# One decoder layer on one core: block inversion moved from VectorE to GpSimd, low parts all on VectorE, gates in one 32-column operand, a second wide group, matmul widths alternating

## The chip, the core and the metric

The kernel runs on one core of a Trainium2 chip. Its time is in microseconds (us) of the device: one execution of the whole program on that core. Three runs of the kernel before took 1485.14, 1487.25 and 1487.25 us, median 1487.25. In this document PE is TensorE, which multiplies matrices; DVE is VectorE; ACT is ScalarE; POOL is GpSimd; SP is the engine that issues most of the DMAs. A lower-case c in the rows is one of 67 general buffers.

## The reference

One decoder layer for 256 tokens of width 2048, all in float32. What matters here:

```python
proj = h @ w_in[l]                      # q, k, v, z, b, a, p
o_gdn = gated_deltanet(qkv, z, b, a, ...)   # 8 heads x 128, in chunks of 64
o_pool = multiscale_pool(p, pool_w[l], pool_scale[l])
mix = jnp.concatenate([o_gdn, o_pool], axis=-1) @ w_out[l]
h = layer_norm(DEEPNORM_ALPHA * h + mix, ...)
xa = memory_cross_attention(h, mem, xq_w[l], xk_w[l], xv_w[l], xo_w[l])
h = layer_norm(DEEPNORM_ALPHA * h + xa, ...)
ff = jnp.square(jax.nn.relu(h @ w_up[l])) @ w_down[l]
h = layer_norm(DEEPNORM_ALPHA * h + ff, ...)
...
# inside gated_deltanet, for each head and chunk:
L = jnp.where(strict, jnp.einsum("nbhcd,nbhmd->nbhcm", k_beta, k) * decay, 0.0)
sol = lax.linalg.triangular_solve(eye + L, rhs, left_side=True, lower=True, unit_diagonal=True)
```

The triangular solve is done with explicit inverses. The smallest ones are of 64 blocks of 32 x 32, one block to a partition; they are built by 31 steps of a multiplication and a subtraction, and that is the "block inversion".

## The kernel before

**Two parts of each operand.** Every float32 operand of a large matmul is split into a high part H, which ACT rounds to the fast matmul type (line 188), and a low part L = x - H, which DVE subtracts (line 189). A product is the sum H·H + H·L + L·H. One weight tile is 128 x 1024 numbers (512 KB), so one tile costs ACT one activation and DVE one subtraction. H and L tiles have 3 buffers each, the raw tile W has 4: ACT can start the split of a tile when PE has finished with the tile three places before it, so that PE has at most three tiles in hand when ACT or DVE stops. Ten of the subtractions (`POOL_W`, plan places 40 to 109, every sixth) go to POOL.

**Wide groups.** A projection group (`proj_a`) gives 512 output columns in four PSUM accumulators, from 8 weight tiles. In the wide form the activations' two parts lie side by side, so that one 512-column matmul does H·H and H·L (line 325) and one 256-column matmul does L·H (line 329). Over a tile PE does all 8 wide ones, then all 8 narrow ones; in a group's last tile it does 2 and 2 for each accumulator. The two halves of a wide accumulator are added afterwards: for most groups ACT copies it out and POOL adds (`fold`, line 203). In the narrow form, which the first two groups have, there are three 256-column matmuls (line 346).

**Groups in order.** The ten groups of `w_in` come first: two of k, two of q, two of v, two of z, two of p. Between the first two stand the gates (`gates_plan`): 48 matmuls with a 128-column weight operand in which only 16 columns are not zero. Then follow the memory's k, `w_out`, the memory's v, the queries `w_q`, `w_o`, and the MLP's up and down projections.

**What sets the order.** The work that is not a projection (convolutions, heads, inversion, solve, normalisation) is a list of generators, the background. After each weight tile `bg.step` runs them until a budget for DVE and ACT is used up (2.35 and 3.4 us a tile), counted by the costs that the generators yield, not by the clock. The order on every engine's queue is fixed when the program is built; each engine works its queue strictly in that order and waits where an operand is missing.

**The inversion.** `base_inverse` (line 709) sends the blocks through memory: eight small DMAs write `ld`, SP loads it as `lb` (line 716), DVE does the 31 steps (lines 726 and 728; step j works on (31-j)(j+1) elements, 5,456 over all steps, twice), SP stores `xd` (line 731), and ACT issues 16 small DMAs that load the result (line 735). Each of these three queues goes on only when the step before it is done. The activation of z (`silu`, line 899) is put two tiles behind the fold that it needs.

Of the kernel before, what the change touches and what calls it, by code (L numbers as in the profile page):

```python
# [15 lines left out]
P = 128  # L16
T = 256
# [30 lines left out]
POOL_W = 40, 110, 6  # L48
# [75 lines left out]
def hybrid_layer(ctx: ExitStack, tc: tile.TileContext, xT, xtok, memT, w_ba, w_in, small, w_pool,  # L124
# [59 lines left out]
    def split(h, l, src, n=0, eng=V):  # L184

        if n:
            bg.charge(.09 + 1.05e-3 * n if eng is V else 0, .1 + .84e-3 * n)
        S.activation(out=h, in_=src, func=AF.Copy)  # L188
        eng.tensor_tensor(out=l, in0=src, in1=h.bitcast(F32), op=ALU.subtract)  # L189
# [34 lines left out]
    def run():  # L224
# [24 lines left out]
        def do_split():  # L249
            i = pos["split"]  # L250
            kind, src, shape, fn = plan[i][:4]
            if kind in "fwh":
                h = wp.tile([P] + shape, F32R, tag="H", name=nm("H"), bufs=HB)
                l = wp.tile([P] + shape, F32R, tag="L", name=nm("L"), bufs=HB)
                split(h, l, raw.pop(i), shape[0] * shape[1] if len(shape) == 2 else 1024,
                      nc.gpsimd if POOL_W[0] <= i < POOL_W[1] and i % POOL_W[2] == 0 else V)
# [55 lines left out]
    def proj_a(src, acts, evac, kt_outer=False, load=None, fine=0, pre=None, wide=False, spread=False):  # L312
        accs = []

        def tile_fn(k0, ns):
            def fn(h, l):
# [6 lines left out]
                def first(s, n):  # L323
                    c = slice(n * P, (n + 1) * P)
                    mm(out=accs[n], lhsT=h[:, s, c], rhs=acts[k0 + s].wide, start=k0 + s == 0, stop=False)  # L325

                def second(s, n):
                    c = slice(n * P, (n + 1) * P)
                    mm(out=accs[n][:, :T], lhsT=l[:, s, c], rhs=acts[k0 + s][0], start=False, stop=k0 + s == KT - 1)  # L329

                if wide:

                    for part in ([[(s, n) for s in range(ns)] for n in range(4)] if last else [order]):
                        for s, n in part:
                            first(s, n)
                        for s, n in part:
                            second(s, n)
# [103 lines left out]
    nc.gpsimd.memset(m64[0:64, 64:128], 1.0)  # L441
    eps_ln = const.tile([P, 1], F32, name="eps_ln")
# [149 lines left out]
    def gates_plan():  # L592
        pb = []

        def fn(j):
            def f(h, l):
                if j == 0:
                    pb.append(acc())
                o = pb[0][:, :T]
                for s in range(8):  # L600
                    kt = 8 * j + s
                    a = xs[kt]
                    mm(out=o, lhsT=h[:, s, :], rhs=a[0], start=kt == 0, stop=False)
                    mm(out=o, lhsT=h[:, s, :], rhs=a[1], start=False, stop=False)
# [902 lines left out]
```

## Time and profile before

| | us |
|---|---|
| median of three runs | 1487.25 |
| the profiled execution | 1487.29 |
| its span | 1485.6 |
| PE busy | 1468.0 |
| DVE busy | 944.8 |
| ACT busy | 726.0 |
| POOL busy | 149.5 |

The span is the time from the first to the last instruction that the profiler saw; 1.7 us of the execution lie outside it. In a timeline a row gives the start, the duration from the first start to the last end, and a count; matmuls overlap, so the distance of two starts, not the duration of one, is what a matmul costs. The value in brackets is the idle time of the engine before the row, and what ended it.

### The profile page before, as it was taken

What the parts mean: (1) busy time and instruction counts of PE and PEld (TensorE: products, weight loads), DVE (VectorE), ACT (ScalarE), POOL (GpSimd) and SP (SyncE); (2) the same over time, 40 slices, a digit from 0 to 9 for tenths busy, and PEclk for the clock granted to TensorE, in tenths of its full rate; (3) what the DMA queues carried; (4) which work ended last, traced back from release to release, by engine and by line L of the source; (5) the groups of instructions that cost most, each with busy time, mean ns of one, the idle gap of its engine ahead of it and who ended that gap; (6) DMA issues with size and microseconds to landing.
All of it is one profiled execution on the core that took longest, in us unless ns stands there. A gap on an engine that the chain in (4) does not pass through costs nothing.

```text
span 1485.6 us, 21126 instructions
## 1 busy us (share of the span) xinstructions
PE 1468.0 (99%) x8038; PEld 1274.6 (86%) x8038; DVE 944.8 (64%) x1471; ACT 726.0 (49%) x1061; POOL 149.5 (10%) x191
## 2 busy tenths in 40 slices
PE   9999999999999999999999999999999999999996
PEld 8988889899888888998888888888888888888886
DVE  6778976867656755555685555566555565556656
ACT  6765555755533545453545444455334444345441
POOL 1024323700300000000130000000000000000001
PEclk9999999999999999999999999999999999999998
DMA  7556555535855555444735655555556655555571
GB/s 273 188 196 184 171 187 173 188 132 170 289 194 194 179 189 189 147 138 156 279 131 176 199 191 189 196 188 181 197 197 204 228 193 191 192 197 185 185 247 65
DMA packets 86758, 280.45 MB, mean 189 GB/s; under 512 B 13904, under 2 KB 14944, under 8 KB 86656
## 3 DMA queue, kind: packets, MB, share of 16 engines
q1 hardware_dynamic: 78928, 268.73, 54.1%
q0 software_dynamic: 2960, 9.58, 2.0%
q10 hardware_dynamic: 4768, 0.79, 0.3%
q8 instruction: 63, 1.03, 0.3%
q14 instruction: 39, 0.32, 0.1%
HBM read 276.43 MB, written 2.63 MB: 188 GB/s over the span
## 4 chain that ended last, share of the span: by engine, by line
PE 97%; DVE 1%; DMA 1%; ACT 1%; issue 0%; POOL 0%; ACTq 0%; POOLq 0%; DVEq 0%
PE acc L325 29%; PE acc L329 15%; PE acc L371 13%; PE acc L373 13%; PE acc L372 13%; PE acc L346 5%; PE acc L408 0%; PE acc L407 0%; PE acc L406 0%; DMA W<-w_in 0%; PE acc L1346 0%; PE acc L1344 0%; PE acc L1345 0%; PE aux L1191 0%; PE aux L1227 0%
## 5 line engine op out<-in xcount | busy, mean ns | idle before, releaser
L189 DVE TENSOR_TENSOR L<-W,H 128x1024 fp32r<-128x1024 f32 x469 | 579.0, 1236 | 465.4 <-ACT H L188 461.7
L188 ACT ACTIVATE H<-W 128x1024 fp32r<-128x1024 f32 x479 | 507.4, 1059 | 587.4 <-PE acc L373 301.5
L325 PE MATMUL acc<-c,H 128*128 128x512 f32 x1920 | 499.5, 394 | 1.1 <-DVE c L189 0.6
L325 PEld LDWEIGHTS acc<-c,H 128*128 128x128 f32 x1920 | 338.3, 189 | 56.8 <-ACT c L200 1.7
L371 PE MATMUL acc<-H,c 128*128 128x512 f32 x832 | 325.3, 391 | 0.0
L373 PE MATMUL acc<-H,c 128*128 128x512 f32 x832 | 323.9, 389 | 0.0
L372 PE MATMUL acc<-L,c 128*128 128x512 f32 x832 | 323.9, 389 | 0.0
L329 PEld LDWEIGHTS acc<-c,L 128*128 128x128 f32 x1920 | 274.2, 190 | 27.2
L329 PE MATMUL acc<-c,L 128*128 128x256 f32 x1920 | 281.4, 282 | 0.0
L373 PEld LDWEIGHTS acc<-H,c 128*128 128x128 f32 x832 | 156.2, 188 | 32.8
L372 PEld LDWEIGHTS acc<-L,c 128*128 128x128 f32 x832 | 156.3, 188 | 31.7
L371 PEld LDWEIGHTS acc<-H,c 128*128 128x128 f32 x832 | 156.2, 188 | 31.8
L203 POOL TENSOR_TENSOR c<-c 128x256 f32<-128x256 f32 x60 | 48.8, 839 | 372.5 <-ACT c L200 372.5
L189 DVE TENSOR_TENSOR c<-c,c 128x256 fp32r<-128x256 f32 (+1 forms) x170 | 76.6, 503 | 10.3 <-ACT c L188 10.3
L188 ACT ACTIVATE c<-c 128x256 fp32r<-128x256 f32 (+1 forms) x170 | 66.5, 455 | 2.5 <-DMA c<-xT 2.5
L346 PE MATMUL acc<-c,H 128*128 128x256 f32 x384 | 66.3, 288 | 1.1 <-ACT H L188 1.1
L1062 POOL DMA_DIRECT2D c<-lnrow x24 | 12.9, 540 | 518.4 <-PE acc L373 345.7
L346 PEld LDWEIGHTS acc<-c,H 128*128 128x128 f32 x384 | 57.8, 196 | 2.1 <-ACT H L188 1.8
L346 PE MATMUL acc<-c,L 128*128 128x256 f32 x192 | 47.6, 287 | 0.0
L200 ACT ACTIVATE c<-acc 128x512 f32<-128x512 f32 x60 | 35.6, 599 | 18.9 <-PE acc L329 15.0
L531 DVE SCALAR_TENSOR_TENSOR c<-c,par 128x255 f32<-128x255 f32 (+2 forms) x72 | 38.1, 538 | 3.6 <-ACT c L528 1.9
L217 ACT ACTIVATE c<-acc 128x256 f32<-128x256 f32 x60 | 23.0, 384 | 23.0 <-PE acc L329 23.0
(241 smaller groups left out, 1005.5 us busy)
## 6 DMA issues: line engine op xcount, KB each, us to landing
W<-w_up SPq DMA_DIRECT2D x127, 512.0 KB, 3.5
W<-w_down SPq DMA_DIRECT2D x120, 512.0 KB, 3.4
W<-w_in SPq DMA_DIRECT2D x76, 512.0 KB, 3.4
W<-w_k SPq DMA_DIRECT2D x32, 512.0 KB, 3.3
W<-w_out SPq DMA_DIRECT2D x32, 512.0 KB, 4.2
W<-w_v SPq DMA_DIRECT2D x32, 512.0 KB, 3.2
W<-w_q SPq DMA_DIRECT2D x32, 512.0 KB, 3.3
W<-w_o SPq DMA_DIRECT2D x24, 512.0 KB, 3.3
```

The source lines that it names most:

```text
L188: S.activation(out=h, in_=src, func=AF.Copy)
L189: eng.tensor_tensor(out=l, in0=src, in1=h.bitcast(F32), op=ALU.subtract)
L200: S.activation(out=ab.rearrange("p s c -> p (s c)"), in_=o, func=AF.Copy)
L203: nc.gpsimd.tensor_tensor(out=r, in0=ab[:, 0, :], in1=ab[:, 1, :], op=ALU.add)
L217: S.activation(out=r, in_=o[:, :T], func=AF.Copy)
L325: mm(out=accs[n], lhsT=h[:, s, c], rhs=acts[k0 + s].wide, start=k0 + s == 0, stop=False)
L329: mm(out=accs[n][:, :T], lhsT=l[:, s, c], rhs=acts[k0 + s][0], start=False, stop=k0 + s == KT - 1)
L346: mm(out=accs[n][:, :T], lhsT=w[:, s, n * P:(n + 1) * P], rhs=acts[kt][x], start=kt == 0 and w is h and x == 0, stop=kt == KT - 1 and w is l)
L371: mm(out=accs[t], lhsT=a[0][:, c], rhs=h, start=kt == 0, stop=False)
L372: mm(out=accs[t], lhsT=a[0][:, c], rhs=l, start=False, stop=False)
L373: mm(out=accs[t], lhsT=a[1][:, c], rhs=h, start=False, stop=kt == KT - 1)
L531: V.scalar_tensor_tensor(out=u[:, sh:], in0=x[:, :T - sh], scalar=w[:, 3 - sh:4 - sh], in1=u[:, sh:], op0=ALU.mult, op1=ALU.add)
```

## The change

Five edits. The 31 steps of the inversion are issued on POOL in place of DVE, and the generator gives the turn back after every 1.8 us of its own counting. All low parts are subtracted by DVE. The gates' operand shrinks to 16 columns, whose high and low parts stand side by side in one 32-column operand: 16 matmuls of 512 columns, then 4 small ones with a matrix of two identities (`twos`) that add up the parts and transpose. The second group of `w_in` becomes wide. From the queries on, a group's tiles take turns (`turn`): a tile that follows one which ended with narrow matmuls starts with narrow ones, but for the first tile of a group.

```diff
-    def split(h, l, src, n=0, eng=V):
+    def split(h, l, src, n=0):
         if n:
-            bg.charge(.09 + 1.05e-3 * n if eng is V else 0, .1 + .84e-3 * n)
+            bg.charge(.09 + 1.05e-3 * n, .1 + .84e-3 * n)
         S.activation(out=h, in_=src, func=AF.Copy)
-        eng.tensor_tensor(out=l, in0=src, in1=h.bitcast(F32), op=ALU.subtract)
+        V.tensor_tensor(out=l, in0=src, in1=h.bitcast(F32), op=ALU.subtract)
...
             kind, src, shape, fn = plan[i][:4]
-            if kind in "fwh":
+            if kind in "wh" and shape == [KT, 16]:
+                h = wp.tile([P, KT, 32], F32R, tag="H", name=nm("H"), bufs=HB)
+                split(h[:, :, 0:16], h[:, :, 16:32], raw.pop(i), KT * 16)
+                parts[i] = (h, None)
+            elif kind in "fwh":
                 h = wp.tile([P] + shape, F32R, tag="H", name=nm("H"), bufs=HB)
                 l = wp.tile([P] + shape, F32R, tag="L", name=nm("L"), bufs=HB)
-                split(h, l, raw.pop(i), shape[0] * shape[1] if len(shape) == 2 else 1024,
-                      nc.gpsimd if POOL_W[0] <= i < POOL_W[1] and i % POOL_W[2] == 0 else V)
+                split(h, l, raw.pop(i), shape[0] * shape[1] if len(shape) == 2 else 1024)
                 parts[i] = (h, l)
...
-                def first(s, n):
+                def first(s, n, ends):
                     c = slice(n * P, (n + 1) * P)
-                    mm(out=accs[n], lhsT=h[:, s, c], rhs=acts[k0 + s].wide, start=k0 + s == 0, stop=False)
-                def second(s, n):
+                    mm(out=accs[n], lhsT=h[:, s, c], rhs=acts[k0 + s].wide, start=k0 + s == 0,
+                       stop=ends and k0 + s == KT - 1)
+                def second(s, n, ends):
                     c = slice(n * P, (n + 1) * P)
-                    mm(out=accs[n][:, :T], lhsT=l[:, s, c], rhs=acts[k0 + s][0], start=False, stop=k0 + s == KT - 1)
+                    mm(out=accs[n][:, :T], lhsT=l[:, s, c], rhs=acts[k0 + s][0], start=False,
+                       stop=ends and k0 + s == KT - 1)
...
                     for part in ([[(s, n) for s in range(ns)] for n in range(4)] if last else [order]):
-                        for s, n in part:
-                            first(s, n)
-                        for s, n in part:
-                            second(s, n)
+                        low = turn and width[0] == "low" and k0 > 0
+                        for step in (second, first) if low else (first, second):
+                            for s, n in part:
+                                step(s, n, step is (first if low else second))
+                        width[0] = "high" if low else "low"
                         if last:
...
     nc.gpsimd.memset(m64[0:64, 64:128], 1.0)
+    twos = const.tile([P, 16], F32, name="twos")
+    V.tensor_tensor(out=twos, in0=ident[:, 0:16], in1=ident[:, 16:32], op=ALU.add)
     eps_ln = const.tile([P, 1], F32, name="eps_ln")
...
     def gates_plan():
-        pb = []
-        def fn(j):
-            def f(h, l):
-                if j == 0:
-                    pb.append(acc())
-                o = pb[0][:, :T]
-                for s in range(8):
-                    kt = 8 * j + s
-                    a = xs[kt]
-                    mm(out=o, lhsT=h[:, s, :], rhs=a[0], start=kt == 0, stop=False)
-                    mm(out=o, lhsT=h[:, s, :], rhs=a[1], start=False, stop=False)
-                    mm(out=o, lhsT=l[:, s, :], rhs=a[0], start=False, stop=kt == KT - 1)
-                if j == 1:
-                    ba.append(chunk([T]))
-                    S.activation(out=ba[0], in_=o, func=AF.Copy)
-                    bg.event("ba")
-            return f
-        for j in range(2):
-            add("w", w_ba[j], [8, P], fn(j))
+        def fn(hl, _):
+            o = acc()
+            for kt in range(KT):
+                mm(out=o[0:32, :], lhsT=hl[:, kt, :], rhs=xs[kt].wide, start=kt == 0, stop=kt == KT - 1)
+            ba.append(chunk([2, T]))
+            S.activation(out=ba[0][0:32].rearrange("p s c -> p (s c)"), in_=o[0:32, :], func=AF.Copy)
+            bg.event("ba")
+        add("w", w_ba, [KT, 16], fn)
...
         for a in range(NT):
-            nc.tensor.transpose(out=pt[:, a * P:(a + 1) * P], in_=ba[0][:, a * P:(a + 1) * P], identity=ident)
+            for s in range(2):
+                mm(out=pt[:, a * 16:a * 16 + 16], lhsT=ba[0][0:32, s, a * P:(a + 1) * P], rhs=twos[0:32, :],
+                   start=s == 0, stop=s == 1)
         yield 0, .2, 1
-        ptv = pt[:, :T].rearrange("p (a c) -> p a c", a=NT)
+        ptv = pt[:, :2 * 16].rearrange("p (a c) -> p a c", a=NT)
         e = small_tile(sh)
...
         u = small_tile(sh)
-        V.tensor_tensor(out=u, in0=ptv[:, :, 32:40],
+        V.tensor_tensor(out=u, in0=ptv[:, :, 8:16],
                         in1=par[:, C_DT:C_DT + 8].unsqueeze(1).to_broadcast([P, NT, HEADS]), op=ALU.add)
...
         yield 0, 0, 2
+        load = 0
         for j in range(31):
...
             t = tb[:, :n * (j + 1)].rearrange("p (n c) -> p n c", n=n)
-            V.tensor_tensor(out=t, in0=lb[:, j, j + 1:32].unsqueeze(2).to_broadcast([NB, n, j + 1]),
-                            in1=xb[:, j, 0:j + 1].unsqueeze(1).to_broadcast([NB, n, j + 1]), op=ALU.mult)
-            V.tensor_tensor(out=xb[:, j + 1:32, 0:j + 1], in0=xb[:, j + 1:32, 0:j + 1], in1=t,
-                            op=ALU.subtract)
-            yield .3 + 2.1e-3 * n * (j + 1), 0, 0
+            nc.gpsimd.tensor_tensor(out=t, in0=lb[:, j, j + 1:32].unsqueeze(2).to_broadcast([NB, n, j + 1]),
+                                    in1=xb[:, j, 0:j + 1].unsqueeze(1).to_broadcast([NB, n, j + 1]), op=ALU.mult)
+            nc.gpsimd.tensor_tensor(out=xb[:, j + 1:32, 0:j + 1], in0=xb[:, j + 1:32, 0:j + 1], in1=t,
+                                    op=ALU.subtract)
+            load += .3 + 4.6e-3 * n * (j + 1)
+            if load > 1.8:
+                load = 0
+                yield 0, 0, 1
         nc.sync.dma_start(out=xd, in_=xb)
...
         bg.add(f"k{h}", k_head(h), f"x{h}")
-    proj_a(w_in[1], xs, conv_evac(4))
+    proj_a(w_in[1], xs, conv_evac(4, True), wide=True)
     bg.add("base", base_inverse(), *[f"k{h}" for h in range(HEADS)])
...
                 bg.event(f"Q{4 * g + n}")
-        proj_a(w_q[g], f1, q_evac, wide=g < 3, kt_outer=g == 0, pre={0: ["ln1_0", "ln1_1"]} if g == 0 else None)
+        proj_a(w_q[g], f1, q_evac, wide=g < 3, turn=True, kt_outer=g == 0, pre={0: ["ln1_0", "ln1_1"]} if g == 0 else None)
         bg.add(f"att{g}", attend(g), *[f"Q{4 * g + n}" for n in range(4)])
...
                     bg.urgent.append(finish(g, rs, hid))
-            proj_a(w_up[4 * qd + g], f2, u_evac, wide=True, spread=True)
+            proj_a(w_up[4 * qd + g], f2, u_evac, wide=True, spread=True, turn=True)
         for g in range(4):
...
     b, a, p = wi[:, 4096:4104], wi[:, 4104:4112], wi[:, 4112:]
-    wba = np.zeros((D, P), wi.dtype)
-    wba[:, 0:8] = b
-    wba[:, 32:40] = a
+    wba = np.concatenate([b, a], axis=1)
     cw = f(conv_w)[0].reshape(4, 3, 8, P)[:, [1, 0, 2]]
```

Line numbers in the rows of the changed kernel are its own: 188 is the subtraction there, 187 the high part, 202 the fold, 541 a convolution's step, 904 the silu of z, 728 and 730 the inversion, 740 the loads of its result.

DVE's queue, inside the inversion. L_ with a number is the low part of one weight tile; tb, lb and xb belong to the inversion; before:

```order
L189 TENSOR_TENSOR L_2031<-W_1914,H_2030 128x1024
L726 TENSOR_TENSOR tb<-lb,xb 64x255
L728 TENSOR_TENSOR xb<-xb,tb 64x15x17
L726 TENSOR_TENSOR tb<-lb,xb 64x252
L728 TENSOR_TENSOR xb<-xb,tb 64x14x18
L726 TENSOR_TENSOR tb<-lb,xb 64x247
```

Now, at the same place (541 is a convolution, 590 to 595 a query head):

```order
L188 TENSOR_TENSOR L_1940<-W_1784,H_1939 128x1024
L541 SCALAR_TENSOR_TENSOR c_1320<-c_1320,par 128x255
L541 SCALAR_TENSOR_TENSOR c_1320<-c_1320,par 128x254
L541 SCALAR_TENSOR_TENSOR c_1320<-c_1320,par 128x253
L188 TENSOR_TENSOR L_1977<-W_1813,H_1976 128x1024
L590 COPY ssq<-aux_1966 128x2
L593 SCALAR_TENSOR_TENSOR c_1059<-aux_1965,cc,c_1059 128x256
L595 SCALAR_TENSOR_TENSOR c_1059<-aux_1965,cc,c_1059 128x128
```

Between two low parts there stood up to ten instructions of the inversion; now there stand convolutions and query heads, which used to come after it.

POOL's queue, around the fold of the first z group (c_2142 and c_2157 there, c_2175 and c_2190 now); before:

```order
L203 TENSOR_TENSOR c_1944<-c_1945 128x256
L189 TENSOR_TENSOR L_2055<-W_1956,H_2054 128x1024
L203 TENSOR_TENSOR c_2142<-c_2143 128x256
L203 TENSOR_TENSOR c_2142<-c_2150 128x256
L203 TENSOR_TENSOR c_2157<-c_2158 128x256
L203 TENSOR_TENSOR c_2157<-c_2165 128x256
L189 TENSOR_TENSOR L_2233<-W_2112,H_2232 128x1024
```

Now:

```order
L728 TENSOR_TENSOR tb<-lb,xb 64x156
L730 TENSOR_TENSOR xb<-xb,tb 64x6x26
L202 TENSOR_TENSOR c_2175<-c_2176 128x256
L202 TENSOR_TENSOR c_2175<-c_2183 128x256
L202 TENSOR_TENSOR c_2190<-c_2191 128x256
L202 TENSOR_TENSOR c_2190<-c_2198 128x256
L728 TENSOR_TENSOR tb<-lb,xb 64x135
L730 TENSOR_TENSOR xb<-xb,tb 64x5x27
L728 TENSOR_TENSOR tb<-lb,xb 64x112
```

The four folds of z stood behind a low part; now 26 of the 31 steps of the inversion stand ahead of them, and five behind.

ACT's queue, from the silu of that z group to the loads of the inverse; before:

```order
L188 ACTIVATE H_2202<-W_2086 128x1024
L899 ACTIVATE c_2142<-c_2142 128x256 x2
L899 ACTIVATE c_2157<-c_2157 128x256 x2
L188 ACTIVATE H_2232<-W_2112 128x1024
L534 ACTIVATE c_614<-c_1143 128x256
L528 ACTIVATE c_1389<-c_1389,par 128x256
L528 ACTIVATE c_1397<-c_1397,par 128x256
L188 ACTIVATE H_2274<-W_2136 128x1024
L188 ACTIVATE H_2299<-W_2176 128x1024
L735 DMA c_1748<-xd 32x4x32
```

Now:

```order
L187 ACTIVATE H_2256<-W_2088 128x1024
L904 ACTIVATE c_2175<-c_2175 128x256 x2
L904 ACTIVATE c_2190<-c_2190 128x256 x2
L797 ACTIVATE c_2008<-aux_2240,sv 128x128
L797 ACTIVATE c_2009<-aux_2240,sv 128x128
L544 ACTIVATE c_2246<-c_1857 128x256
L544 ACTIVATE c_2251<-c_1865 128x256
L187 ACTIVATE H_2289<-W_2129 128x1024
L740 DMA c_1645<-xd 32x4x32
L740 DMA c_1649<-xd 32x4x32
L740 DMA c_1645<-xd 32x4x32
L740 DMA c_1649<-xd 32x4x32
```

In both the silu stands two tiles behind the evacuation. The loads from xd stood behind three more high parts; now they stand behind one, H_2289, which itself stands behind the silu.

## Rows read from the trace of the kernel before

**Rows 1.** The page: busy us by engine (share of the span), instructions.
```profile
PE 1468.0 (99%) x8038; PEld 1274.6 (86%) x8038; DVE 944.8 (64%) x1471; ACT 726.0 (49%) x1061; POOL 149.5 (10%) x191
```

**Rows 2.** Timeline of PE in an up projection: start us, us, what, count.
```profile
1002.09 2.00 PE L325 MATMUL acc<-c,H 128*128 128x512 f32 x8
1003.93 1.11 PE L329 MATMUL acc<-c,L 128*128 128x256 f32 x8
1004.88 2.00 PE L325 MATMUL acc<-c,H 128*128 128x512 f32 x8
...
1007.68 0.63 PE L325 MATMUL acc<-c,H 128*128 128x512 f32 x2
1008.37 0.63 PE L325 MATMUL acc<-c,H 128*128 128x512 f32 x2
```

**Rows 3.** Timeline of PE, 512-column matmuls alone, 54 starts apart.
```profile
699.63 0.39 PE L371 MATMUL acc<-H,c 128*128 128x512 f32 x1
...
711.87 0.39 PE L371 MATMUL acc<-H,c 128*128 128x512 f32 x1
```

**Rows 4.** Timeline of PE: three narrow matmuls from one start to the other.
```profile
36.02 0.40 PE L346 MATMUL acc<-c,H 128*128 128x256 f32 x2
...
36.38 0.40 PE L346 MATMUL acc<-c,H 128*128 128x256 f32 x2
```

**Rows 5.** One window, 145:191.7: line 726 alone, line 728 alone, all engines.
```profile
145.00:191.70 46.70, 19.95 (x31) 1.00 0.52 169
...
145.00:191.70 46.70, 12.11 (x31) 1.00 0.52 169
...
145.00:191.70 46.70, 46.70 (x273) 41.18 (x272) 45.01 (x76) 24.42 (x32) 18.70 (x13) 1.00 0.52 169
```

**Rows 6.** Timeline of POOL: adds of 1024 and of 256 elements.
```profile
116.36 2.40 POOL L189 TENSOR_TENSOR L<-W,H 128x1024 fp32r<-128x1024 f32 x1 [6.34 <-ACT H L188]
...
288.77 2.81 POOL L203 TENSOR_TENSOR c<-c 128x256 f32<-128x256 f32 x4
```

**Rows 7.** Timeline of DVE and POOL where both work at once.
```profile
269.71 2.33 DVE L531 SCALAR_TENSOR_TENSOR c<-c,par 128x255 f32<-128x255 f32 x3
271.84 1.43 POOL L942 TENSOR_TENSOR c<-c 128x256 f32<-128x256 f32 x2
...
282.40 4.44 DVE L189 TENSOR_TENSOR L<-W,H 128x1024 fp32r<-128x1024 f32 x3
284.22 1.54 POOL L942 TENSOR_TENSOR c<-c 128x256 f32<-128x256 f32 x1
```

**Rows 8.** Timeline of DVE and of SP's queue: the inversion's start, its result's store.
```profile
145.13 1.27 DVE L726 TENSOR_TENSOR tb<-lb,xb 64x31 f32<-64x31 f32 x1
...
191.62 0.46 SPq L731 DMA_DIRECT2D xd<-xb  x1
```

**Rows 9.** Timeline of ACT around the first z group, then its loads of the inverse.
```profile
177.73 2.69 ACT L200 ACTIVATE c<-acc 128x512 f32<-128x512 f32 x4 [0.54 <-PE acc L329]
180.32 1.06 ACT L188 ACTIVATE H<-W 128x1024 fp32r<-128x1024 f32 x1
...
182.63 1.32 ACT L899 ACTIVATE c<-c 128x256 f32<-128x256 f32 x4
...
195.01 1.76 ACTq L735 DMA_DIRECT2D c<-xd  x4
```

**Rows 10.** Timeline of PE: one query head's matmuls, then two waits.
```profile
139.43 0.59 PE L575 MATMUL aux<-c 128*128 128x256 f32 x2
...
140.44 1.86 PE L325 MATMUL acc<-c,H 128*128 128x512 f32 x7
...
202.44 0.61 PE L578 MATMUL aux<-ones,c 128*128 128x1 f32 x4 [0.23 <-ACT c L571]
...
206.41 0.98 PE L325 MATMUL acc<-c,H 128*128 128x512 f32 x3 [0.47 <-ACT c L200]
```

**Rows 11.** Timeline of PE at the start, clock not yet granted in full.
```profile
5.58 2.07 PE L346 MATMUL acc<-c,H 128*128 128x256 f32 x8 [1.13 <-ACT H L188]
```

More of the change, by code (lines that the diff above doesn't have):

```diff
@@ L47 @@
 HOLD, KEEP = 3, 1
-POOL_W = 40, 110, 6
 RLA, XLA, RD = 7, 14, 6
@@ L309, in add, with proj_a @@
         plan.append((kind, src, shape, fn, pre, post))
-    def proj_a(src, acts, evac, kt_outer=False, load=None, fine=0, pre=None, wide=False, spread=False):
+    width = ["low"]
+    def proj_a(src, acts, evac, kt_outer=False, load=None, fine=0, pre=None, wide=False, spread=False, turn=False):
         accs = []
@@ L1481, in _layout @@
         "xT": feat(x), "xtok": f(x)[0].reshape(NT, P, D), "memT": feat(mem),
-        "w_ba": wba.reshape(2, 8, P, P).transpose(0, 2, 1, 3),
+        "w_ba": wba.reshape(KT, P, 16).transpose(1, 0, 2),
         "w_in": tiles(np.concatenate([k, q, v, z, p], axis=1)), "small": small, "w_pool": pw,
```

## The prediction, made before the change was run

> **What bounds the kernel now.** I read the page's busy shares first: PE works 1468.0 of 1485.6 us, 99%, every other engine 64% or less [rows 1]. So the end comes earlier only through fewer or cheaper matmuls, or a wait of PE that goes; and anything that leaves PE without a weight tile comes out on the clock in full. Next, what a matmul costs, from distances of starts: 54 of 512 columns in 711.87 − 699.63 = 12.24 us, 226.7 ns each [rows 3]; three of 256 columns in .36 us, 120 ns each [rows 4]. A full wide tile takes 1.84 us for its 8 wide and .95 for its 8 narrow ones, 2.79 together [rows 2]. Then the one stretch where other engines are full: from 145 to 191.7 DVE works 45.0 of 46.7 us, and the inversion's two lines are 19.95 + 12.11 = 32.1 us of it [rows 5]. Last ACT, SP and PE just behind that stretch: the store of the inverse at 191.62, its loads at 195.01, and two short waits of PE [rows 8 to 10].
>
> **The change part by part.** The sum is made against the profiled execution, 1487.29 us (span 1485.6 and 1.7 outside); the median of the runs, 1487.25, is the same number for this purpose.
>
> *Gates.* 48 × .120 = 5.76 us become 16 × .227 = 3.63, −2.1. Four small matmuls take the place of two transposes; four one-column matmuls take .61 us [rows 10]. The new ones are bounded by 0 and about .8; I take +.4, so −1.7 (−2.1 to −1.3).
>
> *Second group wide.* 64 times three narrow matmuls, .360, become one wide and one narrow, 2.79/8 = .349: −.7 us (0 to −.9). Its four evacuations get folds on POOL, counted below.
>
> *Alternating widths.* In a full tile 2.79 us stands against 8 × .2267 + 8 × .120 = 2.774, so a change from narrow to wide and back costs .016 us (the first step alone, 1.84 − 1.814, .026). In a group's last tile two and two take 1008.37 − 1007.68 = .69, the plain sum [rows 2], so nothing goes there. About three changes between full tiles go in each of 18 groups (three of the queries, fifteen up): 54 × .016 = −.9 us, bounds 0 and −1.4. L is now wanted before H every second tile; it lies ready one tile ahead, and where PE never waits for it that costs nothing.
>
> *Two waits of PE,* .23 and .47 us [rows 10], both behind ACT work that follows the inverse: −.7 if ACT comes earlier, 0 if not.
>
> *DVE* loses 32.1 us and gets the ten low parts back, and conv steps and query heads that stood behind the inversion move into its place. That is about as much as it can do there before PE needs it; I cost it at nothing, since the low parts are first in each tile's share and a tile's is 1.5 us of 2.79 even beside a busy POOL (4.44 for three) [rows 7]. Without that cover it would be late by up to the 4 us by which the moved work could exceed the stretch.
>
> These are −1.7 − .7 − .9 − .7 = −4.0: without any new stall 1483.3.
>
> *The inversion on POOL* is the part that decides. POOL's price: 2.40 us for 1024 elements and 2.81/4 = .70 for 256 [rows 6], so 2.2 ns an element and .13 to .17 us an instruction (two in a chain take 1.43 [rows 7]). The first op came at 145.13 [rows 8]; less the gates' gain 143.5. In POOL's queue steps 0 to 25, 5,031 elements twice, stand ahead of the z folds: 10,062 × 2.2 ns = 22.1, and 52 × .17 = 8.9; with four folds of v and four of z at .70, 5.6 together, 36.6 us if POOL is alone. It is not alone. A 256-element add beside a low part takes 1.54 in place of .70, so one low part costs POOL .84 [rows 7]. Fourteen low parts stand in that stretch of DVE's queue: 12 us. A conv step costs POOL little (two adds that begin under the last of three take 1.43, against 1.40): 27 of them 2 us. So the last fold of z ends at F = 143.5 + 36.6 + 14 = 194.1, bounds 180.1 (no contention at all) and 199 (each low part blocks for its whole time, next paragraph).
>
> The Trainium skill, "SBUF — State Buffer", section "SBUF: two separate sides", says that VectorE with two SBUF inputs and GpSimd hold their common port as an exclusive lock for a whole instruction. The rows show a loss of .84 for one low part, where the low part alone would be (4.44 − .70)/3 = 1.25. By that rule 14 × 1.25 = 17.5 in place of 12, F = 199.6.
>
> Who waits for F: ACT. The silu of z waits for the folds, and behind it stand four copies and the high part H_2289. Evacuation of that group was at 177.73 [rows 9]; it moves by −2.4 (gates, second group), by six query heads that now come before it, 140.44 − 139.43 = 1.0 each [rows 10], and .4 of value heads: 181.7. ACT got to the silu 4.9 us after that [rows 9], so 186.6. PE then has three tiles in hand, 8.4 us: it needs H_2289 at 195.0. ACT gives it F + .66 (half of the four silus' 1.32) + 1.5 (four copies, as the silus) + 1.06 [rows 9] = F + 3.2 = 197.3: **PE stands 2.4 us** (none if F is below 191.8). Next: five steps of the inversion on POOL, 3.7 us with their waits, then the store; store to loads 195.01 − 191.62 = 3.4 [rows 8, 9]; four loads' issue 1.76 [rows 9]; two copies .8 and the next high part 1.06: H_2317 at F + 11.0 with some .3 between them. PE has tile H_2289 done at F + 6.2: **4.8 us more**. The following tiles have four loads each ahead of their high part, 1.76 + .8 + 1.06 = 3.6 against PE's 2.79: **.8 more** before the loads are through. Before the change the same loads came after three more high parts, and PE lived on these.
>
> Sum: 1487.29 − 4.0 + 2.4 + 4.8 + .8 = **1491.3, slower**. Its own range, with F by ±3 us (contention .65 to 1.05 a low part, start ±1): 1488 to 1496.
>
> **The rivals.**
> (a) *Hidden.* POOL is done in time, F below 186.8 (then H_2317 at F + 11.0 comes before PE has finished the tile of H_2289, at 195.0 + 2.8 = 197.8): 1483.3, with the small gains at their ends 1481.5 to 1485.5. For it: two lone collisions are all that the rows show of contention, and ACT's lead over PE is reckoned, not read; against it: a low part would have to cost POOL no more than (186.8 − 182.1)/14 = .33, not .84.
> (b) *Half.* F from 187 to 191.5: no wait at the silu, up to 4.7 us at the loads: 1483.5 to 1488.8, about no change; at 189.5 it is 2.7 + .8, 1486.8.
> (c) *Port and clock, on the other side far out.* F is 199.6 and the long stalls cost PE more than themselves: 2.4 + 5.5 = 7.9, 4.8 and .8 us. At the start, before PE's clock is granted in full, eight 256-column matmuls take over .2 us each where .12 is the steady price [rows 11]; 16 such after each of two stalls are 2.8 us. 1483.3 + 13.5 + 2.8 = 1499.6. It decides from about 17 us of contention on. By the page's rule on the port alone, without the clock, the time would be 1496.8.
> (d) *DVE is the bound*: moved conv steps and heads delay low parts: up to 4 us on (a), 1484 to 1487.
>
> **How the numbers follow.** Forecast .45 (1488 to 1496); (a) .20; (b) .18; (c) .10; (d) .07. A difference of .2% (3 us) is about what a measurement can tell from none: faster is below 1484.3, slower above 1490.2. Faster: most of (a) and a little of (b) and (d): .22. Slower: (c) and over three quarters of the forecast, the part with F from 193 on: .47. The rest is same, .31. The range takes (a) without its outer end, and most of (c): 1482.5 to 1498.
>
> **What would show it.** Right: in the new trace POOL's inversion lines, 52 instructions up to the z folds, busy from 143 to about 194, with many ops of 1.5 us or more; ACT idle before the silu line by over 7 us and before the first load by over 5; PE idle of 2 to 3 us near 195 and 4 to 5 near 202; gates as 16 starts .227 apart; in an up projection full tiles of 2.77. Wrong: POOL's ops beside low parts at their lone times, folds ending before 190, or PE without a gap over 1 us between 190 and 215; or a gap that ends on a low part of DVE, which is (d); or matmuls of twice the length behind a gap, which is (c).

## The result: 1496.28 us, slower by .66%

Six runs of the changed kernel took 1494.64 to 1498.28 us, median 1496.28, beside 1486.80 of the kernel before in the same comparison: ratio 1.0066, 95% interval 1.0056 to 1.0076. The prediction said slower, 1491.3, with 1482.5 to 1498 as its range; 1496.28 lies inside that, and .3 us above the 1488 to 1496 that it gave its own forecast. The profiled execution is the 1494.64 one, with a span of 1492.9 us. It is 7.35 us over the profiled execution of before.

The page after (its first part, busy time; it answers to [rows 1]):

```profile
PE 1467.9 (98%) x7948; PEld 1270.0 (85%) x7948; DVE 932.7 (62%) x1419; ACT 722.1 (48%) x1058; POOL 168.2 (11%) x247
```

PE is busy as long as before (1468.0), since the slow work shown below and the time saved on matmuls cancel in this sum: the span is longer by time in which PE stands. TensorE's timeline, where [rows 10] had two waits of .23 and .47:

```profile
193.66 1.11 PE L334 MATMUL acc<-c,L 128*128 128x256 f32 x8
197.75 0.74 PE L794 MATMUL aux<-ident,c 128*128 128x128 f32 x4 [2.97 <-ACT c L544]
199.00 3.61 PE L329 MATMUL acc<-c,H 128*128 128x512 f32 x8 [0.51 <-ACT H L187]
202.40 1.22 PE L334 MATMUL acc<-c,L 128*128 128x256 f32 x8
...
207.86 3.78 PE L329 MATMUL acc<-c,H 128*128 128x512 f32 x8 [4.24 <-ACT H L187]
211.44 1.76 PE L334 MATMUL acc<-c,L 128*128 128x256 f32 x8
213.03 1.98 PE L329 MATMUL acc<-c,H 128*128 128x512 f32 x8
```

Three things are to be seen. PE waits 2.97 and .51 us for ScalarE, does one tile, waits 4.24 us, and the tiles behind either wait are slow. From start to start the eight wide matmuls take 202.40 − 199.00 = 3.40 and 3.58 us where a steady tile has 1.84 [rows 2], and the second tile's narrow ones 1.59 in place of .95. That is 7.7 us of waiting and 1.56 + 1.74 + .64 = 3.9 us of slow work. The windows of the same stretch (length, then busy time and count of PE, PEld, DVE, ACT, POOL, then PE's granted clock, DMA share, GB/s):

```profile
199.00:203.40 4.40, 4.40 (x16) 3.65 (x16) 1.20 (x1) 0.00 (x0) 2.03 (x5) 0.61 0.22 46
...
207.80:213.00 5.20, 5.14 (x16) 4.37 (x17) 2.55 (x3) 3.03 (x6) 0.00 (x0) 0.51 0.55 135
213.00:216.00 3.00, 3.00 (x19) 2.68 (x18) 1.68 (x2) 1.65 (x4) 0.00 (x0) 1.00 0.79 235
```

The granted clock is .61 and .51 behind the waits, 1.00 again at 213: the slow tiles ran at the lower of the two levels, 1.2 GHz, for most or all of that time.

Who waits for whom, ScalarE first (bracket: idle time and what ended it):

```profile
186.41 1.08 ACT L187 ACTIVATE H<-W 128x1024 fp32r<-128x1024 f32 x1
194.41 0.42 ACT L904 ACTIVATE c<-c 128x256 f32<-128x256 f32 x1 [6.93 <-POOL c L202]
...
197.89 1.05 ACT L187 ACTIVATE H<-W 128x1024 fp32r<-128x1024 f32 x1
204.43 1.76 ACTq L740 DMA_DIRECT2D c<-xd  x4
206.24 0.37 ACT L797 ACTIVATE c<-aux,sv 128x128 f32<-128x128 f32 x1 [7.30 <-issue]
...
206.75 1.05 ACT L187 ACTIVATE H<-W 128x1024 fp32r<-128x1024 f32 x1
```

ScalarE starts a high part at 186.41, then stands 6.93 us until the first fold of z, and delivers H_2289 at 197.89 + 1.05. Then it stands 7.30 us at the first four loads of the inverse, which begin at 204.43 and take 1.76 us of its queue, and H_2317 starts at 206.75. PE's waits end with the copies and the high part behind the silu, and with H_2317. GpSimd and VectorE in the middle of the inversion:

```profile
170.19 0.68 POOL L728 TENSOR_TENSOR tb<-lb,xb 64x255 f32<-64x255 f32 x1
170.32 1.64 DVE L188 TENSOR_TENSOR L<-W,H 128x1024 fp32r<-128x1024 f32 x1
...
170.95 1.55 POOL L730 TENSOR_TENSOR xb<-xb,tb 64x255 f32<-64x255 f32 x1
```
```profile
192.33 1.35 POOL L730 TENSOR_TENSOR xb<-xb,tb 64x156 f32<-64x156 f32 x1
193.66 2.77 POOL L202 TENSOR_TENSOR c<-c 128x256 f32<-128x256 f32 x4
...
201.10 0.24 POOL L730 TENSOR_TENSOR xb<-xb,tb 64x31 f32<-64x31 f32 x1
```

One step's subtraction beside a low part takes 1.55 us; the same subtraction without one takes .69 (experiment five, at 166.28). The low part starts at 170.32, ends at 171.96, and takes 1.64 in place of some 1.22; the subtraction ends at 172.50, .54 behind it. So this meeting cost VectorE .42 and GpSimd .86 us. The last fold of z ends at 193.66 + 2.77 = 196.43 and the last step at 201.34.

The edits that were to gain, at their places (TensorE: the kernel's first matmuls; the gates; the first matmuls of the second group; the sums of the gates and what follows them; the first matmuls of the third group; then an up projection):

```profile
5.55 1.22 PE L354 MATMUL acc<-c,H 128*128 128x256 f32 x8 [1.10 <-ACT H L187]
...
28.69 3.86 PE L607 MATMUL acc<-c,H 128*32 128x512 f32 x16
32.39 2.00 PE L329 MATMUL acc<-c,H 128*128 128x512 f32 x8
...
35.27 1.06 PE L622 MATMUL aux<-twos,c 32*128 32x16 f32 x8
36.26 2.12 PE L329 MATMUL acc<-c,H 128*128 128x512 f32 x8
...
56.81 2.00 PE L329 MATMUL acc<-c,H 128*128 128x512 f32 x8
```
```profile
995.84 2.00 PE L329 MATMUL acc<-c,H 128*128 128x512 f32 x8
...
999.59 3.82 PE L329 MATMUL acc<-c,H 128*128 128x512 f32 x16
1003.25 2.08 PE L334 MATMUL acc<-c,L 128*128 128x256 f32 x16
```

The gates take 32.39 − 28.69 = 3.70, 2.06 less than before (30.26 to 36.02). The small matmuls with `twos`, four in the code, are eight in the trace; they take 36.26 − 35.27 = .99, .85 more than the two transposes (38.90 to 39.04 before). The second group takes 24.42, as before (36.02 to 60.45), but with those .85 in it. In the up projections runs of 16 equal matmuls show that the widths alternate; from this group's start to the next one's lie 22.30 us (995.84 to 1018.14), before 22.34 (988.12 to 1010.46): .04 a group, .7 in 18.

The first row is luck of this one execution: eight matmuls in 1.22 us where before, and in every other trace of this study, they take 2.07 or 2.08 [rows 11]. The trace's list of clock grants begins, at 1.00, at 4.66 us here and at 9.11 in the trace of before; before that point nothing is listed, and a window laid there reads 1.00 in either. In the trace of before the matmuls stand .23 us apart from 5.58 to 7.45 and .12 behind 9.62. It made the profiled execution some 1.6 us shorter than the others of the same kernel, which are 1496 to 1498. Why the clock was up earlier in it, no run shows.

### The profile page after: what moved, and what is told of

It is laid out like the page before. It is cut to its first block, busy times and chain, and to the rows that moved or that the text cites. A ratio compares the mean times of both kernels' runs of the same rounds, so it can differ in the third digit from the quotient of the medians.

```text
span 1492.9 us, 20988 instructions
## 1 busy us (share of the span) xinstructions
PE 1467.9 (98%) x7948; PEld 1270.0 (85%) x7948; DVE 932.7 (62%) x1419; ACT 722.1 (48%) x1058; POOL 168.2 (11%) x247
## 4 chain that ended last, share of the span: by engine, by line
PE 92%; POOL 4%; DVE 1%; DMA 1%; issue 1%; ACT 1%; ACTq 0%; POOLq 0%; SPq 0%; DVEq 0%
PE acc L329 28%; PE acc L334 15%; PE acc L379 13%; PE acc L381 13%; PE acc L380 13%; PE acc L354 3%; POOL tb L728 2%; POOL xb L730 2%; PE acc L416 0%; PE acc L415 0%; PE acc L414 0%; POOL c L202 0%; PE acc L1349 0%; PE acc L1351 0%; PE acc L1350 0%
## 5 line engine op out<-in xcount | busy, mean ns | idle before, releaser
L188 DVE TENSOR_TENSOR L<-W,H 128x1024 fp32r<-128x1024 f32 x477 | 594.1, 1246 | 489.9 <-ACT H L187 488.7
L334 PE MATMUL acc<-c,L 128*128 128x256 f32 x1984 | 278.6, 283 | 0.0
L541 DVE SCALAR_TENSOR_TENSOR c<-c,par 128x255 f32<-128x255 f32 (+2 forms) x72 | 42.2, 593 | 2.6 <-ACT c L538 0.9
L354 PE MATMUL acc<-c,H 128*128 128x256 f32 x256 | 41.7, 284 | 1.1 <-ACT H L187 1.1
```

The source lines that it names most:

```text
L188: V.tensor_tensor(out=l, in0=src, in1=h.bitcast(F32), op=ALU.subtract)
L354: mm(out=accs[n][:, :T], lhsT=w[:, s, n * P:(n + 1) * P], rhs=acts[kt][x], start=kt == 0 and w is h and x == 0, stop=kt == KT - 1 and w is l)
L541: V.scalar_tensor_tensor(out=u[:, sh:], in0=x[:, :T - sh], scalar=w[:, 3 - sh:4 - sh], in1=u[:, sh:], op0=ALU.mult, op1=ALU.add)
```

## The experiments

**One: the inversion back on VectorE, all else as changed.**

```diff
-            nc.gpsimd.tensor_tensor(out=t, in0=lb[:, j, j + 1:32].unsqueeze(2).to_broadcast([NB, n, j + 1]),
+            V.tensor_tensor(out=t, in0=lb[:, j, j + 1:32].unsqueeze(2).to_broadcast([NB, n, j + 1]),
...
-            if load > 1.8:
...
+            yield .3 + 2.1e-3 * n * (j + 1), 0, 0
```

> The changed kernel with only the inversion's 62 instructions issued on VectorE again (and its old turns of the background). Theory: all of the loss comes from the inversion standing on GpSimd in front of the folds and loads that ScalarE waits for. Then the gaps of 3.0, .5 and 4.2 us of TensorE between 194 and 208 us and the half clock behind them (1.6 and 2.4 us) go, the other edits keep about 3 us, and the time is 1482 to 1485.5 us. Rival A, low parts: that all of them are on VectorE delays it, so that a stall of several us stays near the inversion: 1487 to 1492. Rival B, widths: the alternation or the gates cost time somewhere: also above 1487, with distances of starts longer than before in the up projections.

Measured: 1491.86 (1491.79 to 1493.20), ratio to before 1.0036 (1.0023 to 1.0049). The waits near 200 were gone, but there was another:

```profile
373.03 0.38 PE L911 MATMUL aux<-ident,c 128*128 128x128 f32 x2
378.95 0.45 PE L911 MATMUL aux<-ident,c 128*128 128x128 f32 x1 [5.54 <-DVE c L883]
```

TensorE waits 5.54 us at the heads' transposes for VectorE's scaling (L883), and the next matmuls stand behind them in its queue. What the theory expected fell: with the inversion gone from GpSimd and the waits near 200 gone, another loss stands in their place. The time is rival A's, the low parts, but not the place: the wait is at 373, not near the inversion. Experiments seven and eight show that the low parts bring it.

**Two and three: the queues of the two waits, one at a time. Four: both.** In two, VectorE adds the first z group's halves out of PSUM; in three, store and loads of the inverse are issued on GpSimd.

```diff
+            if g == 0:
+                S.activation(out=z, in_=o[:, :T], func=AF.Copy)
+                V.tensor_tensor(out=z, in0=z, in1=o[:, T:], op=ALU.add)
...
-        nc.sync.dma_start(out=xd, in_=xb)
+        nc.gpsimd.dma_start(out=xd, in_=xb)
...
-                S.dma_start(out=Dm[2 * a + g]...
+                nc.gpsimd.dma_start(out=Dm[2 * a + g]...
```

> The changed kernel with the four folds of the first z group added by VectorE, out of PSUM, in place of GpSimd: ScalarE's silu no longer waits for 26 steps of the inversion, but its loads of the inverse still wait for the whole of it. Theory (two waits in a row, each with its own price): the gap before 198 us goes, the inversion ends 2.8 us earlier because four folds are out of its queue, and one gap remains, 6 to 7 us, since TensorE now reaches the tile behind the loads earlier; half the clock loss goes. 1491 to 1494 us. Rival (the silu wait is the whole cause, the second gap only its echo): no gap over 1 us is left, 1483 to 1486.

> The changed kernel with the store of the inverse and its sixteen loads issued on GpSimd's own queue, behind the inversion; the silu still waits for the folds. Theory: the first gap (3.5 us with its half clock of 1.6) stays, the second (4.2 us and 2.4 us of clock) goes: 1488 to 1491 us. Rival (GpSimd's sixteen issues are slow and the block products behind them come late): a new wait of TensorE at the 128-column products behind the loads, 1492 or more.

> Both: z folds of the first group on VectorE, store and loads of the inverse on GpSimd's queue, the inversion still on GpSimd. Theory: ScalarE waits for nothing of the inversion, TensorE has no gap over 1 us between 190 and 215 us, and the time is that of the changed kernel less 7.7 us of gaps and 4 us of clock: 1482.5 to 1486 us, as with the inversion on VectorE. Rival (contention on VectorE's and GpSimd's port, low parts late): gaps stay that end on a low part of VectorE, 1488 or more.

Measured: 1493.38, 1491.17 and 1491.91 us (ratios 1.0042, 1.0030, 1.0031, intervals 1.0025 to 1.0059, 1.0019 to 1.0042, 1.0021 to 1.0040). TensorE's waits, from the traces of two, three and four:

```profile
188.25 2.12 PE L329 MATMUL acc<-c,H 128*128 128x512 f32 x8 [3.31 <-DVE c L901]
190.20 1.11 PE L334 MATMUL acc<-c,L 128*128 128x256 f32 x8
...
206.81 3.62 PE L329 MATMUL acc<-c,H 128*128 128x512 f32 x8 [3.62 <-ACT H L187]
```
```profile
199.65 0.74 PE L794 MATMUL aux<-ident,c 128*128 128x128 f32 x4 [2.98 <-ACT c L544]
200.90 3.38 PE L329 MATMUL acc<-c,H 128*128 128x512 f32 x8 [0.51 <-ACT H L187]
```
```profile
187.88 2.14 PE L329 MATMUL acc<-c,H 128*128 128x512 f32 x8 [3.26 <-DVE c L901]
```

Three did as its theory said, at a time .2 us above its 1488 to 1491: 2.98 and .51 stay, the second wait is gone, and so is the clock loss behind it. The two waits can be taken away one by one. Two took the silu's wait away and put another in its place: at 188.25 TensorE waits 3.31 us for VectorE's add, since the next group's accumulators come free only when it has read them, and it stands behind a convolution and a low part. Behind it TensorE is late itself, so that the second wait is 3.62 where 6 to 7 were expected. Four has the first of these alone, up to 340 us; its profiled execution, 1488.52, is the fastest of its ten. What was expected of the z edit missed it in both.

The record shows one thing more. Behind this wait the clock did not fall. In two, from the wait on (window as above):

```profile
188.20:191.20 3.00, 2.96 (x17) 2.60 (x18) 2.93 (x6) 0.53 (x3) 2.61 (x6) 1.00 0.61 180
```

The granted clock is 1.00, and the eight wide matmuls take 190.20 − 188.25 = 1.95 us; in four, behind 3.26 us, 1.98. In three, behind 2.98 and .51, they take 204.08 − 200.90 = 3.18. So a wait of 3 us is not always followed by slow matmuls, and its length alone does not tell which.

**Five: no low parts while the inversion runs.**

```diff
+                if 63 <= i < 77:
...
+                    S.activation(out=h, in_=raw.pop(i), func=AF.Copy)
+                    parts[i] = (h, h)
...
```

> The changed kernel without the 14 low parts that VectorE computes while the inversion runs on GpSimd; TensorE reads the high part in their place, so the products of those 14 weight tiles are not those of the reference (left out: the subtraction). Everything else stands in the same order. Theory, contention: each of the 14 costs GpSimd .84 us, so the last fold before the silu ends near 184 to 186 us in place of 196.4, the inversion 12 us earlier, no gap over 1 us between 190 and 215 us, and the time is 1482 to 1486. Rival, GpSimd's own pace: the folds end within 2 us of 196.4, and both gaps stay, 1492 or more.

A line not shown charges the planner for both instructions as before, so that the order of the others stays. Measured: 1484.57 in its one run, and between 150 and 350 us no two starts of TensorE lie over .2 us further apart than their matmuls need. GpSimd:

```profile
145.64 0.66 POOL L734 TENSOR_TENSOR tb<-lb,xb 64x31 f32<-64x31 f32 x1 [4.05 <-DMA lb<-ld]
...
166.28 0.69 POOL L736 TENSOR_TENSOR xb<-xb,tb 64x255 f32<-64x255 f32 x1
...
182.00 0.56 POOL L736 TENSOR_TENSOR xb<-xb,tb 64x156 f32<-64x156 f32 x1
183.46 2.83 POOL L202 TENSOR_TENSOR c<-c 128x256 f32<-128x256 f32 x4 [0.90 <-ACT c L199]
...
190.56 0.45 POOL L736 TENSOR_TENSOR xb<-xb,tb 64x31 f32<-64x31 f32 x1
```

The 26 steps ahead of the z folds, with the four folds of v between them, take 182.56 − 145.64 = 36.9 us; in the changed kernel, whose first step starts at 143.73, they take 193.68 − 143.73 = 49.95. That is 13.0 us for 14 low parts, .93 each. GpSimd now even waits .90 us for the z copies. So it is the meeting with the low parts that makes GpSimd late; at its own pace it would have been in time.

**Six: matmuls on zeros in the two gaps.**

```diff
+            if t in (76, 77):
+                keep_warm(7 if t == 76 else 9)
```

> The changed kernel with matmuls on zeros put into TensorE's two gaps: 7 of .427 us (3.0) ahead of the first, 9 (3.8) ahead of the second, less than the gaps last. Theory: what follows a gap runs at half clock because TensorE stood idle; kept busy it runs the two tiles behind at 227 ns a start, the clock loss of 1.6 and 2 to 2.4 us goes, the gaps themselves stay, 1492 to 1494 us. Rival (the slow starts have another cause, the weight loads or the late high parts): starts of 427 ns stay behind both gaps, 1495.5 to 1498.

```profile
196.71 3.18 PE L471 MATMUL aux<-warm 128*128 128x256 f32 x14
...
200.84 2.08 PE L331 MATMUL acc<-c,H 128*128 128x512 f32 x8 [0.51 <-ACT H L187]
202.76 1.11 PE L336 MATMUL acc<-c,L 128*128 128x256 f32 x8
208.72 5.77 PE L471 MATMUL aux<-warm 128*128 128x256 f32 x18 [4.85 <-ACT c L799]
```
```profile
199.00:203.70 4.70, 4.19 (x25) 3.44 (x23) 1.22 (x1) 1.79 (x4) 3.57 (x9) 1.00 0.00 0
...
208.70:212.20 3.50, 3.48 (x9) 2.82 (x10) 1.23 (x1) 1.79 (x3) 0.00 (x0) 0.52 0.46 95
```

Measured: 1500.39 (ratio 1.0092, 1.0078 to 1.0105), slower than either expected, yet in the first gap it tells the two apart. There the fillers ran (seven in the code, 14 in the trace), the granted clock stayed 1.00, and the tile behind took 202.76 − 200.84 = 1.92 where the changed kernel has 3.40. In the second they waited for an accumulator that ScalarE still had to read, stood 4.85 us with everything else, and then ran themselves at .52, 5.77 us long, behind the gap and not in it. So behind the first gap the lower clock came of TensorE's standing idle, and not of anything else that is late there; the second gap was not filled and says nothing on it.

**Seven: inversion on VectorE and the ten low parts on GpSimd; gates, wide group and alternation stay.** (The inversion as in one; `POOL_W` and `eng` as in the kernel before.) **Eight: the kernel before with all low parts on VectorE.**

```diff
-POOL_W = 40, 110, 6
+POOL_W = 0, 0, 6
```

> The changed kernel with the inversion on VectorE and the ten low parts on GpSimd, both as before: what stays of the change are the gates, the second wide group and the alternation. Theory formed after the run with the inversion alone put back: with all low parts and the inversion on VectorE its budget is overdrawn by about 10 us, the heads come late, and the group behind waits 5.7 us for them near 373 us; the budget eased, that gap goes. 1482.5 to 1485.5 us, no gap over 1 us. Rival (something else of the change delays the heads): the gap near 373 stays at several us, 1489 or more.

> The kernel before with only one edit, all low parts on VectorE. Theory (the budget of the background): the heads finish some tiles later and TensorE waits 4 to 7 us at their transposes behind the memory's first groups, 1490 to 1494 us. Rival (ten subtractions of 1.2 us are lost in VectorE's slack): within 1 us of before, 1486 to 1488.

Seven: 1486.25 (1484.51 to 1488.33), ratio 1.0002 (.9993 to 1.0011). Eight: 1492.22, ratio 1.0042 (1.0025 to 1.0059), with the wait at the heads again:

```profile
375.52 0.30 PE L909 MATMUL aux<-ident,c 128*128 128x128 f32 x1 [0.49 <-DVE c L881]
379.26 1.75 PE L909 MATMUL aux<-ident,c 128*128 128x128 f32 x7 [3.44 <-DVE c L881]
```

So low parts on VectorE are by themselves a loss of 6 us, through the heads. Is it VectorE's time or the number that the planner counts? **Twelve** moves the ten subtractions and leaves their count at nothing, so that all else stands where it stood.

```diff
-        eng.tensor_tensor(out=l, in0=src, in1=h.bitcast(F32), op=ALU.subtract)
+        V.tensor_tensor(out=l, in0=src, in1=h.bitcast(F32), op=ALU.subtract)
```

> The kernel before with all low parts on VectorE, but the ten that used to go to GpSimd counted at nothing in the background's budget, so that every other instruction stands where it stood before. Theory (the counted budget made the heads late in the run with all low parts on VectorE, 1492.2 us): the gaps of .5 and 3.4 us near 375 go; what stays is VectorE's own time, four subtractions of 1.2 us more inside the inversion, a gap of 0 to 4 us near 200: 1486 to 1490. Rival (VectorE's time itself, not the count): heads still late, gaps of 3 us or more near 375, 1491 to 1494.

Measured: 1486.01 (1484.07 to 1486.46), ratio .9994 (.9985 to 1.0003). The heads' wait is gone, no new one came near 200, and of the .67 that the solve waited before, .32 is left:

```profile
291.83 1.16 PE L820 MATMUL aux<-c,c 128*128 128x128 f32 x8 [0.32 <-DVE c L814]
```

It was the count: ten times .09 + 1.05e-3 × 1024 = 1.17 us, 11.7 in all, off a budget of 2.35 a tile puts the background back. The heads' last scaling begins at 368.91 before, at 378.34 in eight and at 367.42 in twelve. VectorE itself had room.

**Nine and ten: a way to keep the inversion on GpSimd.** ScalarE copies the whole accumulator and VectorE adds from the copy, for the first z group (nine) and for both (ten); store and loads on GpSimd as in three.

```diff
+            ab = chunk([2, T])
+            S.activation(out=ab.rearrange("p s c -> p (s c)"), in_=o, func=AF.Copy)
...
+            V.tensor_tensor(out=z, in0=ab[:, 0, :], in1=ab[:, 1, :], op=ALU.add)
```

> The changed kernel, inversion on GpSimd, store and loads of the inverse on GpSimd's queue, and the first z group's accumulators copied out whole by ScalarE and added by VectorE from the copies. Theory: the run with VectorE adding out of PSUM lost 3.3 us because the accumulators came free only behind a convolution and a low part; now ScalarE frees them at once, no gap over 1 us is left up to 340 us, and the time is 1483 to 1487. Rival (VectorE itself is too late at that place): a gap of 2 us or more near 185 to 200 that ends on VectorE, 1488 to 1491.

> As the run with the first z group copied out and added by VectorE, now for the second z group too, so that no silu stands behind GpSimd's queue; inversion, store and loads of the inverse on GpSimd. Theory: the gap of 3.0 us at 216 (silu behind folds that stood between GpSimd's sixteen loads) goes with its .8 and .9 us of clock, and no gap over 1 us is left up to 340 us: 1483 to 1487. Rival (the inverse itself is late now): a gap of several us at the block products or the solve behind 220 us, 1488 to 1493.

Nine: 1491.15 (ratio 1.0035, 1.0024 to 1.0046). The wait at 188 went, and the next stood at 219.55, by the same chain one group later: GpSimd issues twelve of sixteen loads, then the folds, and ScalarE's silu stands behind them.

```profile
207.54 4.40 POOL L740 DMA_DIRECT2D c<-xd  x8 [4.18 <-DMA xd<-xb]
...
213.28 2.17 POOL L740 DMA_DIRECT2D c<-xd  x4 [1.34 <-DMA c<-xd]
215.46 2.77 POOL L202 TENSOR_TENSOR c<-c 128x256 f32<-128x256 f32 x4
216.24 0.42 ACT L912 ACTIVATE c<-c 128x256 f32<-128x256 f32 x1 [5.32 <-POOL c L202]
...
219.55 0.44 PE L794 MATMUL aux<-ident,c 128*128 128x128 f32 x2 [2.99 <-ACT c L544]
```

Ten took that away too: 1486.79 (1484.23 to 1488.35), ratio 1.0000 (.9991 to 1.0009), no wait of TensorE over 1 us up to 340 us (one of 1.62 stands at 351.50). With the inversion, all low parts and the other edits left as in the change, the loss is gone once ScalarE waits there for nothing in GpSimd's queue: that shows the cause. So the inversion can stand on GpSimd at no loss, and at no gain that the runs can tell.

**Eleven: the alternation alone, in the kernel before** (`proj_a` and `turn=True` as in the change).

> The kernel before with the alternating widths alone, from the queries on. Theory: each wide group becomes .04 to .05 us shorter, 18 of them, .6 to .9 us in all, nothing else moves; 1485 to 1486.5, which the runs can hardly tell from before, but the group's starts can. Rival (the low part is wanted earlier and TensorE waits for it): a group is as long as before or longer, with waits on VectorE in the up projections.

Measured: 1485.89, ratio .9999 (.9990 to 1.0008). From the wait near 558 us, which all traces have, to the last matmul it has 1472.8 − 558.5 = 914.3 us, before 1473.2 − 558.3 = 914.9: the .6 to .7 is in the trace, and within the runs' scatter.

No version here was faster than the kernel before by more than its interval.

## Why the prediction was right, and where its sizes were not

**The mechanism was right, step by step.** Folds of z behind 26 steps: forecast end 194.1, measured 196.43. For the 14 low parts it had 12 us and experiment five has 13.0; the rest of the 2.3 us lies in GpSimd's other work and its start. Behind it ScalarE, then TensorE: first wait 2.4 forecast, 2.97 + .51 measured; second 4.8, measured 4.24; the .8 more behind it did not show. Together 8.0 against 7.7. Experiment three shows that the second can go while the first stays.

**The contention.** The Trainium skill ("SBUF — State Buffer", section "SBUF: two separate sides") has the port that VectorE and GpSimd share as an exclusive lock for a whole instruction. The trace agrees in kind: in the pair above each instruction lasts longer by a good part of the other, .42 and .86 us. In size it lies below the 17.5 us that the prediction worked out for that rule: .93 a low part, 13.0 us in all. In that pair the subtraction ends .54 us behind the low part where alone it takes .69, so some .15 of it is not added; that this holds for all 14 is not shown. That the 1496.8 us which rival (c) has for the port alone lies nearest to 1496.28 is chance: it is made of 13.5 us of waits and no loss of clock, and measured are 7.7 and 3.9.

**The step that failed on size: "PE stands 2.4 us ... 4.8 us more" was priced as the waits alone.** The forecast left TensorE's clock at full behind them and put its loss into rival (c), at 2.8 us and a chance of .10. It is 3.9 us: in the trace both waits are followed by the lower clock, and experiment six shows for the first that the idle wait brings it. With it the forecast's own sum would have been 1495.2. The price of slow matmuls stood in the rows, at the start of the kernel [rows 11]; whether a wait is followed by them did not, and experiments two and four have one that is not.

**The gains were too large: −4.0 forecast.** The traces have −1.2 for the gates (−2.06, and +.85 for the small matmuls, where I took +.4 with .8 as the bound, and compared four with what are eight in the trace), −.9 for the second group and −.7 for the alternation, 2.8 together with the forecast's −3.3. The two waits of .23 and .47, and .67 at the solve, went, 1.9 us from start to start; but two of .9 and .6 came at 360 and 387, where the background stands in another order. Experiment seven, these edits alone, is 1.0002 of before: −1.0 to +1.6 us. The span of its profiled execution is 2.3 us shorter than that of before (1483.3 and 1485.6); the runs together can't show what is left of that.

**The sum of the profiled executions.** 7.7 of waits, 3.9 of clock, −2.8 of matmuls, some −.4 of small waits, −1.6 of luck at the start make +6.8; measured is +7.35, and .5 is not assigned. The median is 9.5 over that of before: the 1.6 of luck is in one execution only, and the profiled execution of before lies .5 above its median.

**A right answer with a wrong reason: VectorE at nothing.** I let the ten low parts cost nothing as VectorE had lost 32 us of inversion. In the changed kernel that held; rival (d) did not come. But the cover was not VectorE's time. It was the planner's count (what `bg.step` spends), which lost 31 × .3 + 2.1e-3 × 5,456 = 20.8 us for the inversion and gained 11.7: experiments one and eight, where the inversion's count stays, lie 5 and 6 us above before with a wait at the heads, and twelve, with the work of eight uncounted, loses nothing. For the changed kernel this is worked out from these three; no run gives it back the inversion's count alone.

**Open.** In the traces of six and ten some 2 us more of TensorE's waits stand in the normalisation near 755 to 785 us than in the others, at instructions that are the same in all; executions of four, seven and nine scatter by 4 to 7 us. I did not find out what sets it. In four and nine the clock goes with it: the mean granted clock of the fastest execution is .996 and .997 (1488.52 and 1487.06 us), that of the slowest .994 in both (1493.54 and 1493.77). What decides whether the clock falls behind a wait is open. Whether seven or twelve is faster than before by 1 to 2 us stays open too.

## What to carry to other kernels

Before work is moved to an idle engine, list what already stands in that engine's queue behind the place, and who waits for that on an engine that feeds the busiest one: here the lateness of four adds and sixteen loads cost more than 32 us of freed VectorE time gave. A wait of the matmul engine is to be priced with the slow matmuls that can follow it, 3.9 us here beside 7.7 of waiting, as a range: they did not follow every wait. And where a planner spends counted costs, an edit of the counts is an edit of the whole order: undo the work and the count separately before either is blamed.

## What the runs showed of the hardware

A wait of TensorE of 3.0 + .5 us was followed by 3.4 us, one of 4.24 by 5.2 us at the lower granted clock (.61 and .51 over the windows), and matmuls on zeros in the first gap prevented it there (experiment six). A wait of 3.31 us in experiment two and one of 3.26 in four were followed by the full clock. A low part on VectorE (1.22 us alone) and a step's subtraction on GpSimd (.69 alone) that meet take 1.64 and 1.55; 14 low parts made GpSimd 13.0 us later. A load issued on GpSimd takes .55 us of its queue (4.40 for eight); the sixteen of experiment nine take 4.40 + 2.17 + 2.17 = 8.74, with a wait of 1.34 and the four folds between them.
